# A hybrid decoder layer: the triangular inverse from 16x16 blocks, four gates moved, attention's values channel-major

## The chip, the cores and the metric

The kernel runs on one core of a Trainium2 chip. The metric is the device time of one execution in microseconds (us), as the median of several runs. The engines are TensorE (PE in the profile; its weight loads are PEld), VectorE (DVE), ScalarE (ACT), GpSimd (POOL) and the queue engine SyncE (SP), which issues the loads and stores.

## The reference

One layer, 512 tokens, width 1024, all in fp32:

```python
h = rms_norm(x, norm1_w) * (1 + sc1) + sh1
att_in, rwkv_in, gate_in = split(h @ w_in)
y_att  = attention_mixer(att_in) @ w_att_out
y_rwkv = rwkv7_mixer(rwkv_in, ...) @ w_rwkv_out
g_att, g_rwkv = split(sigmoid(gate_in + b_gate))
x = x + gt1 * ((g_att * y_att + g_rwkv * y_rwkv) @ w_o)
x = x + gt2 * conv_ffn(rms_norm(x, norm2_w) * (1 + sc2) + sh2, ...)
return rms_norm(x, norm_f_w)
```

The attention has 8 heads of 64 channels and three patterns (window and dilation); their results are joined per head by the softmax denominators. In this kernel the patterns are held as two groups: group 0 is the plain window, group 1 both dilated ones. The RWKV mixer has 16 heads of 64 channels. Per token and head its state is multiplied by a decay, corrected by a rank-one term and increased by another; the kernel does this in chunks of 64 tokens, which needs, per chunk and head, the inverse of a unit-triangular 64x64 matrix.

## The kernel before

**Products.** A large product in fp32 is done as three products of rounded halves (hi x hi, hi x lo, lo x hi), each with 512 moving columns. One block of 128 output channels over 1024 inputs is a "body" of 24 such matmuls (`body`). Its weights are loaded, rounded by ACT (`whi`) and the remainder taken by DVE (`wlo`). Small fp32 products run as they are.

**The order of the work.** From the first projections to the end of the mixers the order on each engine is written out by a planner (`Plan.run`, L93). Each task has an engine, an estimated duration, what it depends on, a priority and named buffers that it takes and gives (`take`, `give`). The planner plays the tasks through in time and issues them in that order; on the chip each engine then runs its instructions strictly in that order. Small and urgent PE tasks have low priority numbers (`C_`, `S_`); the units of bodies have `U_` plus their number, so they fill what is left, in the order in which they were made. Bodies write into two PSUM buffers, called `mm`.

**Attention** (`attention`, `attend`). For each block of queries: scores on PE (`sc`), masked minimum on DVE, exponentials on ACT (`pr`), a turn on PE (`pt`), a copy (`pts`), and the product with the values on PE (`po`, function `values`): stationary is the turned probability tile of 128x128, moving are 64 columns of values, so that the result has tokens in partitions. At the end (from L985) each group's share per token and head (`ea`) scales the result on DVE (`scale`, L1017), 32 transposes bring it into channel order and add the two groups in PSUM (`pa<-ident,o`), ACT copies it, and it is stored to `att_d`. During attention DVE also sums up the rest of the conditioning (`ada_rest`: rows of `w_ada` are loaded into `araw` and added into `acc`, L347), and PE adds each sum over the partitions (`ada`).

**The RWKV mixer** (`rwkv`, from L1041). The 16 heads are 8 pairs (`pair`), two pairs make a group, four groups g = 0 to 3. Per group: two pairs, then `inverse(g)`, then `chain(g)` of 8 steps. Pairs of groups 0 and 2 share buffers (`gp0`), and so do 1 and 3 (`gp1`): group 2's pairs start after chain 0 and group 3's after chain 1. Chains follow each other.

**The inverse** (from L1436). Of each 64x64 matrix the two 32x32 diagonal blocks are inverted on DVE for all four blocks and 16 matrices at once: matrices lie in partitions, `turned` transposes, `scaled` multiplies by the inverse norms, and then columns 30 down to 3 are done two at a time (`two`, L1507: a multiply, a reduction and a correction) and the last three singly (`step`, L1500), over rows of up to 32 elements. `rows` and `rows11` turn the result back; two blocks of small matmuls (`first_pe`, `second_pe`, 32 products each of 32x32 with 32 columns, names `pe`) form the off-diagonal block.

**The chain.** In a step, `state` multiplies the carried state (`mbd`) and then the new values with `gt` into `xy`; `state_out` multiplies `mbd` into `xo`; then come solve (`u`), update and output.

**The gates.** 16 bodies (`early_gate`, m = 0 to 15), made after all pairs: the product, a tanh on ACT (`gs`), a store to DRAM (`gate_d`). When all tasks marked `pre` are done (pairs, gates and their stores), `close_pre` closes the pairs' buffers (pool `pp`) and opens those that follow; `gates` (L1818) loads gates 0 to 7 back. After chain 2, `close_even` opens the buffers for `att_out` (L1853): it loads `att_d`, splits it and runs 8 bodies of 12 matmuls (`pa<-ahi,whi` and so on), the results of which are multiplied with gates 0 to 7. `rwkv_ahead` begins the product `pr`. Then follow `rwkv_out`, the mix, and the feed-forward part.

Of the kernel before, what the change touches and what calls it, by code (L numbers as in the profile page):

```python
# [128 lines left out]
class Layer:  # L129
# [502 lines left out]

    def mask2(self):
# [38 lines left out]
    def attention(self):  # L672
# [4 lines left out]
        o = [ap.tile([P, 4, ATT_W], F32, name="o0"), None]  # L677
# [110 lines left out]
        def attend(gi, hf, order, blocks, width, mask, V, ready, prio):  # L788
# [4 lines left out]
            for n, i, new, end in order:  # L793
# [37 lines left out]
                def values(n=n, i=i, d=d, new=new, end=end):  # L831
                    if new:
                        pos[n] = self.aps.tile([P, 256], F32, tag="po", name=self.n("po"), bufs=2)
                    vs = V(n)
                    for h in range(2):
                        cs = slice(i * P + h * 64, i * P + h * 64 + 64)
                        for j, v in enumerate(vs):
                            self.mm(pos[n][:, cs], d["pts"][:, h, j * P : (j + 1) * P], v[:, cs],
                                    new and h == 0 and j == 0, end and h == 1 and j == len(vs) - 1)

                def out(n=n, i=i, new=new):
                    c0, c1 = (i * P if new else 0), i * P + P
                    if gi and o[1] is None:
                        o[1] = ap.tile([P, 4, ATT_W], F32, tag="o1", name="o1")
                    nc.scalar.copy(o[gi][:, n, hf * 256 + c0 : hf * 256 + c1], pos[n][:, c0:c1])
# [11 lines left out]
                t = pe(0.9 * wd / 256, values, [t], S0, take=("po",) if new else (), give=("pts",), name="po")  # L857
# [110 lines left out]
        for _ in ada:  # L968
            pass

# [23 lines left out]
        scaled = []  # L994
        for gi in range(2):
# [19 lines left out]
            def scale(n, gi=gi, ea=ea):  # L1015
                ov = o[gi][:, n, :].rearrange("p (h e) -> p h e", h=8)
                nc.vector.tensor_tensor(ov, ov, ea[:, n, :].unsqueeze(2).to_broadcast([P, 8, 64]), op=ALU.mult)  # L1017
            t = dve(0.6, diff, [got[gi], *stats[gi]], name="al")
            t = sca(0.45, exps, [t], name="al")
            t = dve(1.2, share, [t], name="al")  # L1020
            scaled += [dve(0.7, lambda n=n, scale=scale: scale(n), [t, *outs[gi]], name="al") for n in range(4)]
        for i in range(4):
            d = {}

            def turn(i=i, d=d):
                d["pa"] = self.aps.tile([P, S], F32, tag="pt", name=self.n("pa"), bufs=2)
                for n in range(4):
                    self.tr(d["pa"][:, n * P : (n + 1) * P], o[0][:, n, i * P : (i + 1) * P], n == 0, False)
                for n in range(4):
                    self.tr(d["pa"][:, n::4], o[1][:, n, i * P : (i + 1) * P], False, n == 3)  # L1030

            def out(d=d):
                d["t"] = self.awl.tile([P, S], F32, tag="attT", name=self.n("attT"), bufs=2)
                nc.scalar.copy(d["t"], d["pa"])
            t = pe(0.95, turn, scaled, take=("pt",), name="pa")
            t = sca(0.6, out, [t], take=("attT",), give=("pt",), name="pa")
# [4 lines left out]
    def rwkv(self, tail):  # L1041
# [17 lines left out]
        def half():  # L1059
# [3 lines left out]
                                    op=ALU.add)  # L1063
        self.opened = pl.add("NO", 0, open_, list(pl.tasks), name="open")
# [6 lines left out]
        for g in range(4):  # L1071
# [3 lines left out]
            self.chain(g)  # L1075
        for m in range(2 * KD):
            self.early_gate(m)
# [358 lines left out]
    def inverse(self, g):  # L1436
# [15 lines left out]
        quads = [(e, b, (64 if e == 0 else 0) + 32 * b) for b in range(2) for e in range(2)]  # L1452

# [4 lines left out]
        def recip():  # L1458
            rn = d["rn"] = pp.tile([P, 32], F32, tag="rn", name=self.n("rn"))
            nc.vector.transpose(rn, d["sq"].rearrange("p s y -> p (s y)"))  # L1460
            nc.vector.tensor_scalar(rn, rn, 1e-24, 0.0, op0=ALU.max, op1=ALU.add)
            nc.vector.reciprocal(rn, rn)

        def blocks(j):

            if j == 0:
                d["ld"] = pp.tile([P, 16, 32], F32, tag="lr", name=self.n("ld"))
            e, b, x = quads[j]
            nc.scalar.copy(d["ld"][x : x + 32], blk(e, b, b))

        def turned():
            d["lt"] = pp.tile([P, 32, 32], F32, tag="lt", name=self.n("lt"))
            nc.vector.transpose(d["lt"].rearrange("p j i -> p i j"),
                                d["ld"].rearrange("p y i -> p i y").unsqueeze(2).to_broadcast([P, 32, 2, 16]))

        def scaled():
            lt = d["lt"]
            nc.vector.tensor_tensor(lt, lt, d["rn"].unsqueeze(2).to_broadcast([P, 32, 32]), op=ALU.mult)

        def diagonal():  # L1480
            f = d["lt"].rearrange("p a b -> p (a b)")
            nc.vector.memset(f[:, ::33], 1.0)

            d["sup"] = pp.tile([P, 14], F32, tag="sup", name=self.n("sup"))
            nc.vector.tensor_copy(d["sup"], f[:, 100::66])
            nc.vector.memset(f[:, 100::66], 0.0)

        def first():

            d["both"] = pp.tile([P, 512 + 784], F32, tag="lr", name=self.n("tt"))  # L1490
            f = d["both"][:, :512]
            d["t"] = f.rearrange("p (a b) -> p a b", b=32)
            nc.gpsimd.memset(f, 0.0)
            for x in range(2):
                nc.gpsimd.tensor_scalar(f[:, x : x + 34 * 15 + 1 : 34], d["rn"][:, x::2],
                                        self.half[:, x : x + 1], 0.0, op0=ALU.mult, op1=ALU.add)

        tmp = lambda *n: d["both"][:, 512 : 512 + math.prod(n)]

        def step(j):  # L1500
            n0 = (j + 1) // 2
            sh = [P, 16 - n0, 32 - j]
            t, x = d["t"], tmp(*sh[1:]).rearrange("p (n i) -> p n i", i=32 - j)
            nc.vector.tensor_tensor(x, t[:, n0:, j:], d["lt"][:, j, j:].unsqueeze(1).to_broadcast(sh), op=ALU.mult)
            nc.vector.tensor_reduce(t[:, n0:, j], x, axis=AX.X, op=ALU.add)

        def two(j):  # L1507

            n0 = j // 2
            sh = [P, 16 - n0, 2, 32 - j]  # L1510
            t, x = d["t"], tmp(*sh[1:]).rearrange("p (n c i) -> p n c i", c=2, i=32 - j)
            nc.vector.tensor_tensor(x, t[:, n0:, j:].unsqueeze(2).to_broadcast(sh),
                                    d["lt"][:, j - 1 : j + 1, j:].unsqueeze(1).to_broadcast(sh), op=ALU.mult)
            nc.vector.tensor_reduce(t[:, n0:, j - 1 : j + 1], x, axis=AX.X, op=ALU.add)
            nc.vector.scalar_tensor_tensor(t[:, n0:, j - 1], t[:, n0:, j], d["sup"][:, j // 2 - 2 : j // 2 - 1],
                                           t[:, n0:, j - 1], op0=ALU.mult, op1=ALU.add)

        def rows():

            d["tc"] = tmp(16, 32).rearrange("p (a b) -> p a b", b=32)  # L1520
            nc.vector.transpose(tmp(16, 32).rearrange("p (z y n s) -> p z n s y", z=1, s=2, n=16)[:, 0], d["t"])

        def rows11():

            d["t11"] = d["lt"][:, :16]
            nc.vector.transpose(d["t11"], d["tc"])

# [7 lines left out]
        t = dve(2.06, turned, lds)  # L1535
        t = dve(1.24, scaled, [t, rn])
        t0 = pl.add("POOL", 2.6, first, [t, self.halved], E_)
        t = dve(0.6, diagonal, [t])
        cost = lambda n, j: n * (16 - (j + 1) // 2) * (32 - j) / 480
        t = pl.join([t, t0])  # L1540
        for j in range(30, 2, -2):
            t = dve(0.55 + cost(2, j), lambda j=j: two(j), [t], name=f"inv{g}")
        for j in range(2, -1, -1):
            t = dve(0.37 + cost(1, j), lambda j=j: step(j), [t], name=f"inv{g}")
        tc = dve(1.1, rows, [t], E_)
        t11 = dve(0.72, rows11, [tc], E_)
# [3 lines left out]
        def first_pe():  # L1550
            pe = d["pe"] = self.cps.tile([P, 512], F32, tag="t", name=self.n("pe"))
# [12 lines left out]
        p1 = pl.add("PE", 1.25, first_pe, [t11], 0.5, take=("t",), name="pe")  # L1564
# [7 lines left out]
    def chain(self, g):  # L1572
# [42 lines left out]
        for c in range(NCH):  # L1615
# [9 lines left out]
            def state(c=c, s=s, gt=gt, R=R, X=X, ih=ih):  # L1625
                xy = s["xy"] = ps("xy")
                s["uv"] = uvs[c - c % 2][:, c % 2]
                for i in range(2 if c else 0):
# [49 lines left out]
            so_ = pe(0.33 if c else 0.0, state_out, [st], C_ + 0.01, take=("xo",), name="xo")  # L1678
# [26 lines left out]
        for i in range(2):  # L1705
# [43 lines left out]
            t = pe(1.05, gate, [t, self.sgs], S_, take=("t",), give=("g2",), name="gg")  # L1749
            gt_ = sca(0.6, gate_out, [t], E_, take=("gg",), give=("t",))  # L1750
# [67 lines left out]
    def gates(self, opened):  # L1818
# [4 lines left out]
        def load(m):  # L1823
            self.p[m] = self.pp2.tile([P, S], F32, name=f"gate{m}", tag=f"gate{m}")
            nc.sync.dma_start(self.p[m], self.gd[m])
        for m in range(KD):
# [347 lines left out]
```

## Time and profile before

| | us |
|---|---|
| runs | 1234.05, 1231.15, 1232.48 (median 1232.48) |
| profiled execution | 1231.16 |
| its span, first to last instruction | 1229.4 |
| mean granted clock of TensorE | 0.982 |
| attention, from the first `po` to the last | 77 to 321 |
| chain 0, 1, 2, 3 | 444 to 490, 516 to 560, 644 to 688, 708 to 752 |
| feed-forward, from its first product | 857 |

A row of the timeline has the start, the time and the engine, line, operation and tiles (out<-in) with the shape: for a matmul "128*64 128x512" is the stationary side (rows*columns) and the moving one. In brackets stands the idle time before it and what ended that. A row of the groups ends in the count, the busy time in us, the mean in ns and the idle time before. Matmuls overlap, so the time that one holds PE is the distance to the next start, not its own length.

### The profile page before, as it was taken

The numbers are of one execution on the slowest core, as the hardware profiler recorded it, in microseconds if no ns is written. First come the engines' busy times: TensorE is split into PE (matmuls) and PEld (weight loads), VectorE is DVE, ScalarE is ACT, GpSimd is POOL, SyncE is SP. The second block draws the span as 40 slices with busy tenths as digits, with TensorE's granted clock in tenths as the row PEclk, the third lists the DMA queues.
The fourth block names the chain that finished last, engine by engine and source line by source line (L and its number), as shares of the span: only waits on it lengthen the run. The fifth ranks groups of instructions, "written<-read, shape, count | busy, mean of one in ns | idle before, by whom it ended". The sixth has DMA issues, their size and how long they took to land.

```text
span 1229.4 us, 18443 instructions
## 1 busy us (share of the span) xinstructions
PE 1179.8 (96%) x7188; PEld 946.3 (77%) x7188; DVE 746.0 (61%) x1254; ACT 542.6 (44%) x1009; POOL 120.3 (10%) x235
## 2 busy tenths in 40 slices
PE   4999999999999999999999599999999999999997
PEld 3788888889777876767776467788888888878886
DVE  6687862431678977846896844665556555652135
ACT  4384621522566364464544443444444444442123
POOL 4000000000001013131103122214000000000001
PEclk9899999999999999999999699999999999999999
DMA  9845871130233332413231525560232323333331
GB/s 317 248 142 157 284 236 46 52 86 5 81 100 84 98 108 72 127 44 116 78 99 49 159 60 177 154 206 18 69 103 86 103 86 103 86 103 103 103 120 69
DMA packets 168902, 139.41 MB, mean 113 GB/s; under 512 B 8849, under 2 KB 150251, under 8 KB 168815
## 3 DMA queue, kind: packets, MB, share of 16 engines
q1 hardware_dynamic: 168671, 137.98, 37.0%
q8 instruction: 56, 0.92, 0.3%
q14 instruction: 31, 0.25, 0.1%
q10 hardware_dynamic: 144, 0.26, 0.1%
HBM read 127.65 MB, written 10.56 MB: 112 GB/s over the span
## 4 chain that ended last, share of the span: by engine, by line
PE 82%; DVE 9%; DMA 4%; ACT 2%; issue 1%; SPq 0%; POOL 0%; POOLq 0%; DVEq 0%; ACTq 0%
PE u L148 22%; PE o L148 13%; PE v L148 7%; PE pg L148 7%; PE qk L148 6%; PE pr L148 3%; PE r L148 3%; PE k L148 3%; PE pa L148 3%; DMA araw<-in_w_ada_dram 2%; PE early L148 2%; PE po L148 2%; PE xy L148 2%; PE pt L151 1%; PE xo L148 1%
## 5 line engine op out<-in xcount | busy, mean ns | idle before, releaser
L194 DVE TENSOR_TENSOR wlo<-raw,whi 128x1024 fp32r<-128x1024 f32 x67 | 83.9, 1252 | 152.6 <-ACT whi L193 152.6
L148 PE MATMUL u<-h2lo,whi 128*128 128x512 f32 (+2 forms) x368 | 142.3, 387 | 0.0
L148 PE MATMUL u<-h2hi,whi 128*128 128x512 f32 (+2 forms) x368 | 142.2, 387 | 0.0
L148 PE MATMUL u<-h2hi,wlo 128*128 128x512 f32 (+2 forms) x368 | 142.2, 386 | 0.0
L1136 ACT CAST whi<-raw 128x1024 fp32r<-128x1024 f32 (+2 forms) x73 | 72.5, 994 | 122.7 <-PE qk L148 49.5
L193 ACT CAST whi<-raw 128x1024 fp32r<-128x1024 f32 x67 | 70.3, 1049 | 112.1 <-PE o L148 53.8
L1139 DVE TENSOR_TENSOR wlo<-raw,whi 128x1024 fp32r<-128x1024 f32 (+2 forms) x73 | 83.7, 1149 | 19.1 <-ACT whi L1136 18.8
L148 PEld LDWEIGHTS u<-h2lo,whi 128*128 128x128 f32 x368 | 68.9, 187 | 15.8 <-POOL h2lo L405 0.2
L148 PEld LDWEIGHTS u<-h2hi,wlo 128*128 128x128 f32 x368 | 68.9, 187 | 15.7
L148 PEld LDWEIGHTS u<-h2hi,whi 128*128 128x128 f32 x368 | 68.9, 187 | 15.4
L2019 DVE SCALAR_TENSOR_TENSOR u<-u,cols,u 128x511 f32<-128x511 f32 x88 | 65.7, 746 | 4.3 <-ACT u L2017 2.7
L148 PE MATMUL qk<-hhi,wlo 128*128 128x512 f32 x160 | 64.0, 400 | 0.0
L148 PE MATMUL qk<-hlo,whi 128*128 128x512 f32 x160 | 63.6, 397 | 0.0
L148 PE MATMUL qk<-hhi,whi 128*128 128x512 f32 x160 | 63.5, 397 | 0.0
L148 PE MATMUL o<-whi,fhi 128*128 128x512 f32 x144 | 56.1, 390 | 0.3 <-DVE u L2019 0.3
L148 PE MATMUL o<-whi,flo 128*128 128x512 f32 x144 | 56.0, 389 | 0.0
L148 PE MATMUL o<-wlo,fhi 128*128 128x512 f32 x144 | 56.0, 389 | 0.0
L148 PE MATMUL pg<-hhi,wlo 128*128 128x512 f32 x128 | 51.8, 405 | 0.0
L148 PE MATMUL pg<-hlo,whi 128*128 128x512 f32 x128 | 51.7, 404 | 0.0
L148 PE MATMUL pg<-hhi,whi 128*128 128x512 f32 x128 | 51.7, 404 | 0.0
L810 DVE CUSTOM_DVE_ANT_0 sm<-sc,m 128x256 f32<-128x256 f32 (+1 forms) x64 | 23.9, 404 | 37.6 <-PE sc L148 36.5
L347 DVE SCALAR_TENSOR_TENSOR acc<-araw,cols,acc 128x1024 f32<-128x1024 f32 x28 | 35.9, 1281 | 15.9 <-DMA araw<-in_w_ada_dram 15.8
(409 smaller groups left out, 2779.1 us busy)
## 6 DMA issues: line engine op xcount, KB each, us to landing
raw<-in_w_in_dram SPq DMA_DIRECT2D x62, 512.0 KB
raw<-in_w_up_dram SPq DMA_DIRECT2D x44, 512.0 KB
araw<-in_w_ada_dram SPq DMA_DIRECT2D x32, 512.0 KB
raw<-in_w_down_dram SPq DMA_DIRECT2D x22, 512.0 KB
araw<-in_w_ada_dram SPq DMA_DIRECT2D x32, 256.0 KB
wvraw<-in_w_in_dram SPq DMA_DIRECT2D x20, 256.0 KB
gate_d<-gs SPq DMA_DIRECT2D x16, 256.0 KB
gate<-gate_d SPq DMA_DIRECT2D x16, 256.0 KB
```

Of the source, the lines that this page charges most:

```text
L148: return self.nc.tensor.matmul(out, lhsT, rhs, start=start, stop=stop)
L151: self.nc.tensor.matmul(out, in_, self.ident[: in_.shape[0], : in_.shape[0]], is_transpose=True, start=start, stop=stop,)
L193: self.nc.scalar.copy(hl[0], raw)
L194: (lo_eng or self.nc.vector).tensor_tensor(hl[1], raw, hl[0], op=ALU.subtract)
L347: nc.vector.scalar_tensor_tensor(d["acc"], raw, ck, d["acc"], op0=ALU.mult, op1=ALU.add)
L810: nc.vector.tensor_tensor_reduce(d["sm", h][:, :wd], d["sc"][h][:, :wd], m[:, 256 - wd : 256] if gi == 0 else m[:, :wd], 1.0, 3.0e38, op0= ...
L1136: nc.scalar.copy(d["w"][0], d["raw"])
L1139: nc.vector.tensor_tensor(d["w"][1], d["raw"], d["w"][0], op=ALU.subtract)
L2019: nc.vector.scalar_tensor_tensor(u[:, d:], pu[:, : S - d], ch(c), u[:, d:], op0=ALU.mult, op1=ALU.add)
```

## The change

It has four parts.

**The inverse.** DVE now inverts the four 16x16 diagonal blocks of each 64x64 matrix. `two` runs six times (columns 14 to 4) and `step` three times, over at most 16 elements. `turned` handles half as many elements. Two blocks of 64 products each (`half_pe`, 32x32 stationary with 16 moving columns), each followed by an ACT copy, and a further transpose join them to 32x32 blocks; then `first_pe` and `second_pe` follow as before.

```diff
-        for j in range(30, 2, -2):
-            t = dve(0.55 + cost(2, j), lambda j=j: two(j), [t], name=f"inv{g}")
+        for j in range(14, 2, -2):
+            t = dve(0.55 + 2 * (16 - j) ** 2 / 480, lambda j=j: two(j), [t], name=f"inv{g}")
...
-        t11 = dve(0.72, rows11, [tc], E_)
+        t = [dve(0.27, wide0, [t], E_), sca(0.42, wide1, [t], E_)]
+        tc = dve(1.1, rows, t, E_)
+        t = dve(0.72, rows11, [tc], E_)
+        for j in range(2):
+            t = pl.add("PE", 1.6, lambda j=j: half_pe(j), [t, ey], 0.5, take=() if j else ("t",), name="pe")
+            tc = t = sca(0.42, lambda j=j: half_out(j), [t], 0.5, name="pe")
+        t11 = dve(0.72, rows11, [tc], 0.5)
...
+        def half_pe(j):
...
+            for y in range(16):
+                for e, b, x in quads:
+                    r = slice(x, x + 32)
+                    l, t = (part("lr", 512, 32)[r, y], d["tc"][r, y, 16:]) if j else (blk(e, b, b)[:, y], d["t11"][r, y, :16])
+                    self.mm(d["pe"][r, 256 * j + 16 * y : 256 * j + 16 * y + 16], l, t, y == 0, y == 15)
```

**Four gates.** Gates 4 to 7 are no early gates any more. Their bodies are made in `gates`, after all others of the pairs, and ACT writes them into their last place once the pairs' buffers are closed; the store and the load fall away.

```diff
+        self.late = range(4, KD)
         for m in range(2 * KD):
-            self.early_gate(m)
+            if m not in self.late:
+                self.early_gate(m)
...
+            if m in self.late:
+                t, d = self.body("gate", self.gate_w(m), KD, "mm", lambda: self.mmp("pg"), self.hT)
+                self.pt[m] = self.pl.add("ACT", 0.7, lambda m=m, d=d: here(m, d), [t, opened], E_, give=("mm",))
+            else:
...
```

**The state in one go.** In `state` the products with `gt` come first and those with `mbd` last, and `state_out` has the highest priority behind them. The gate of `chain` takes its buffer `gg` with the product instead of with the copy.

```diff
                 for i in range(2 if c else 0):
-                    self.mm(xy[X[i], :P], prs[i]["ar"][:, c, X[i]], mbd(i), True, False)
-                for i, h, cs, ci in ih:
-                    self.mm(xy[X[i], cs], gt(i, h, R[i], X[i]), s["uv"][R[i], ci], c == 0 and h == 0, h == 1)
+                    self.mm(xy[X[i], :P], prs[i]["ar"][:, c, X[i]], mbd(i), False, True)
...
-            so_ = pe(0.33 if c else 0.0, state_out, [st], C_ + 0.01, take=("xo",), name="xo")
+            so_ = pe(0.24 if c else 0.0, state_out, [st], C_ - 1.0, take=("xo",), name="xo")
```

**Attention's values.** `values` has 64 columns of values stationary and the 128 probabilities moving, the two heads in the two halves of the partitions, so the result comes out with channels in partitions. The shares per token and head are turned on PE, split in two halves (`hi`, `lo`) and spread over the 64 channels of each head by a product with a pattern of ones (`share_rows`, written by POOL); DVE multiplies, POOL adds the two groups, and the 32 transposes and the ACT copies at the end fall away.

```diff
-                            self.mm(pos[n][:, cs], d["pts"][:, h, j * P : (j + 1) * P], v[:, cs],
-                                    new and h == 0 and j == 0, end and h == 1 and j == len(vs) - 1)
+                    for j, v in enumerate(vs):
+                        for h in range(2):
+                            c0 = i * P + h * 64
+                            self.mm(pos[n][h * 64 : h * 64 + 64, i * P : i * P + P], v[:, c0 : c0 + 64],
+                                    d["pts"][:, h, j * P : (j + 1) * P], new and j == 0, end and j == len(vs) - 1)
...
+            def turn(gi, i=i, d=d):
+
+                d["w", gi] = self.aps.tile([P, S], F32, tag="pt", name=self.n("pw"), bufs=2)
+                self.mm(d["w", gi], self.heads[:, i * P : (i + 1) * P], self.share[gi], True, True)
...
+                nc.gpsimd.tensor_tensor(d["t"], o[0][:, i, :], o[1][:, i, :].rearrange("p (r j) -> p j r", r=4), op=ALU.add)
```

More of the change, by code (lines that the diff above doesn't have):

```diff
@@ L631, in masks, with share_rows @@
                 pattern=[[-1, P]], channel_multiplier=1)
+    def share_rows(self):
+        nc = self.nc
+        self.heads = self.awl.tile([P, 2, S], F32R, tag="qk12", name="heads", bufs=1)[:40, 0, :]
+        t = self.awl.tile([P, 2, S], F32R, tag="qk02", name="share", bufs=1)[:40]
+        self.share = [t[:, gi, :] for gi in range(2)]
+        one = lambda r, c: self.ident[r, c : c + 8].unsqueeze(2).to_broadcast([r.stop - r.start, 8, 64])
+        h = self.heads.rearrange("p (h e) -> p h e", e=64)
+        for r, c in ((slice(0, 32), 0), (slice(32, 40), 32)):
+            nc.gpsimd.tensor_copy(h[r], one(r, c))
+        for x in self.share:
+            nc.gpsimd.tensor_copy(x[:32].rearrange("p (h e) -> p h e", e=64), one(slice(0, 32), 64))
     def mask2(self):
@@ L969, in attention @@
             pass
+        heads = pl.add("POOL", 3.0, self.share_rows, sc, E_, take=("qk02", "qk12"), name="heads")
         def pre():
@@ new lines, in attention, with turn, hi, lo @@
+        parts = []
+        for gi in range(2):
+            d = {}
+            def turn(gi=gi, d=d):
+                d["ps"] = self.aps.tile([P, S], F32, tag="pt", name=self.n("pe"), bufs=2)
+                for n in range(4):
+                    self.tr(d["ps"][:8, n * P : (n + 1) * P], shares[gi][1][:, n, :], n == 0, n == 3)
+            def hi(gi=gi, d=d):
+                nc.scalar.copy(self.share[gi][:8], d["ps"][:8])
+            def lo(gi=gi, d=d):
+                nc.vector.tensor_tensor(self.share[gi][32:40], d["ps"][:8], self.share[gi][:8], op=ALU.subtract)
+            t = pe(0.48, turn, [shares[gi][0], heads], take=("pt",), name="pa")
+            t = sca(0.6, hi, [t], name="pa")
+            parts.append(dve(0.7, lo, [t], give=("pt",), name="pa"))
@@ L1037, in attention @@
+            t = pl.add("POOL", 1.2, out, ts, E_, take=("attT",), name="pa")
             pl.add("DMA", 0.8, lambda i=i, d=d: nc.sync.dma_start(self.att_d[:, i, :], d["t"]), [t], W_, lag=2.0,
@@ L1452, in inverse @@
         quads = [(e, b, (64 if e == 0 else 0) + 32 * b) for b in range(2) for e in range(2)]
+        a0, a1 = [lambda s=s: self.half[:, s : s + 1] for s in range(2)]
+        part = lambda t, c, n: d[t][:, c : c + 16 * n].rearrange("p (y n) -> p y n", n=n)
         def norms():
@@ L1507, in two @@
-        def two(j):
[L1509 to L1516, printed above, removed]
+            sh = [P, 15 - j, 16 - j]
```

148 lines of the change are left out of this document (83 added, 65 removed).

## The prediction

> **What bounds the kernel now.** I read the page's share by engine and its slices first, then the windows, the timeline around the one hole, and the groups by shape.
>
> ```profile
> span 1229.4 us, 18443 instructions
> PE 1179.8 (96%) x7188; PEld 946.3 (77%) x7188; DVE 746.0 (61%) x1254; ACT 542.6 (44%) x1009; POOL 120.3 (10%) x235
> PE   4999999999999999999999599999999999999997
> PEclk9899999999999999999999699999999999999999
> ```
>
> TensorE (PE) is full in every slice but the first, the last and number 23, where the granted clock falls too. So a microsecond counts only if it is PE work, or falls into a hole of PE. Two windows size that hole (columns: us, busy PE, PEld, DVE, ACT, POOL, clock, DMA share, GB/s):
>
> ```profile
> 682.00:712.00 30.00, 16.89 (x213) 12.20 (x215) 24.01 (x43) 13.34 (x29) 3.93 (x5) 0.54 0.63 184
> 712.00:742.00 30.00, 30.00 (x298) 19.96 (x298) 12.29 (x26) 13.27 (x39) 7.85 (x16) 1.00 0.16 45
> ```
>
> Between 682 and 712 us PE is busy 16.89 us at a clock of 0.54, which is 16.89 x 0.54 = 9.1 us of full-clock work: 30 - 9.1 = 20.9 us are lost. The rows of that place say why (timeline, and the rows of single lines and tiles):
>
> ```profile
> L1816 ACT ACTIVATE gs<-pg,b_gate x16: 674/682/693, 425.2 to 681.3; 128x512 f32<-128x512 f32 x16
> 655.00:697.20 42.20, 0.00 (x0) 0.00 (x0) 22.06 (x50) 2.47 (x4) 1.47 (x3) 0.85 0.35 111
> L1841 SPq DMA_DIRECT2D ld<-att_d x4: 319/375/430, 685.2 to 698.0; - x4
> 687.92 0.97 PE L148 MATMUL xo<-uv,gt 128*64 128x64 f32 x8 [0.36 <-ACT uv L1654]
> 693.31 0.48 PE L151 MATMUL t<-ident,yt 128*128 128x128 f32 x1 [3.58 <-POOL yt L1801]
> 705.82 1.12 PE L148 MATMUL u<-cen,v 128*64 128x128 f32 x8 [3.03 <-DVE u L1589]
> 706.87 0.80 PE L148 MATMUL pa<-ahi,whi 128*128 128x512 f32 x1
> ```
>
> The last of the 16 early gates is evicted at 681.3; they were the filler of PE. The inverse of group 3 occupies VectorE until 697 (second row: instructions on tile tt alone, 22.06 us of DVE), so chain 3 begins only at 705.8, though chain 2 issued its last products at 687.9. The output projection of attention (pa) needs its loads, issued 685.2 to 698.0, and begins at 706.9, 19 us after chain 2. Three suppliers fail at once.
>
> **The change part by part.** All times are against the profiled execution, 1231.16 us: its span of 1229.4 and 1.8 around it. The median of the three runs, 1232.48, lies 1.3 above.
>
> *Late gates and shorter inverse: the hole.* Rows by shape for the inverse, and a gate's pace:
>
> ```profile
> L1473 DVE STREAM_TRANSPOSE lt<-ld 128x1024 f32<-128x1024 f32 x4 | 8.1, 2037 | 1.2 <-ACT ld L1469 1.2
> L1512 DVE TENSOR_TENSOR tt<-tt,lt 128x256 f32<-128x256 f32 x4 | 1.7, 425 | 0.1
> L1514 DVE TENSOR_REDUCE tt<-tt 128x16 f32<-128x256 f32 x4 | 1.7, 421 | 0.1
> L1515 DVE SCALAR_TENSOR_TENSOR tt<-tt,sup 128x10 f32<-128x10 f32 x4 | 1.0, 238 | 0.1
> L1512 DVE TENSOR_TENSOR tt<-tt,lt 128x4 f32<-128x4 f32 x4 | 0.6, 160 | 0.1
> 433.14 0.39 PE L148 MATMUL pg<-hhi,whi 128*128 128x512 f32 x1
> 433.37 0.39 PE L148 MATMUL pg<-hlo,whi 128*128 128x512 f32 x1
> ```
>
> The 14 steps of two columns and 3 single ones shrink from up to 784 elements to at most 288: six steps of two and three single ones. From the rows (0.16 us at 4 elements, 0.425 at 256) a multiply averages 0.28, a reduction the same, the correction 0.24: 6 x (0.28 + 0.28 + 0.24) + 3 x 2 x 0.37 = 7.0 us, against some 20 of the 22.06 (two closing transposes are in it). The first transpose, over 1024 elements, halves (-1), the scaling after it loses a third of its 1.2 and the extra small ones add 1.5. DVE is left with about 12 us per inverse where it had 25 (22.06 + 2.04 + the scaling); the new round trips (two blocks of matmuls, two ACT copies, one more transpose) give back some 5 of latency. Each inverse ends about 8 us sooner, and chain 3 can follow chain 2 at once. A gate is 24 matmuls at 0.23 us = 5.5; four of them, 22 us of PE work, now run without a store and a load and do not hold back the moment when the pairs' buffers close. Eight DMA issues leave SP. In the gap of some 19 us from chain 2's end to pa there are now chain 3 and up to 22 us of gates. I count 19 of the 20.9 us as won. What is late next is nothing on that path: PE work itself. Bounds: 0 to -21.
>
> *Joining the 16x16 blocks.* Eight new blocks of 64 products each, fp32, so 128 matmul records (this trace shows two records for each fp32 product). Nearest row, the existing joining step with 32 products:
>
> ```profile
> 433.96 1.20 PE L148 MATMUL pe<-lt,gt 32*32 32x32 f32 x64 [0.20 <-DVE lt L1526]
> 435.09 0.50 PE L148 MATMUL pg<-hhi,wlo 128*128 128x512 f32 x1
> ```
>
> 64 records hold PE for 435.09 - 433.96 = 1.13 us. Half as wide a moving side (16) could halve that, or not touch it; four positions instead of two could overlap, or not. Full price by records: 8 x 2 x 1.13 = 18.1, less the 8 x 0.13 of setting up that a block pays once = 17. Low end: 128 records in the time of 64, 8 x 1.13 = 9. I take 17, the row as it stands, and 2 us more for waits (each block waits for DVE or ACT; the 0.20 in the row is one such wait). The Trainium skill, "TensorE: Matmul & The Clock Gate", section "Wait — 56ns, not 53.3ns?", states that start-to-start stays at or above about 25 ns however narrow the moving side is; by it 16 columns cost what 32 cost and the term is 17, which speaks against this part. No row here has 16 columns.
>
> *Attention's values.* Stationary and moving sides change places: 128x64 against 128x128, the two heads in different column halves. That shape exists already (u<-cen,v):
>
> ```profile
> 317.19 1.00 PE L148 MATMUL po<-v,pts 128*128 128x64 f32 x8
> 318.00 0.47 PE L148 MATMUL lg<-hhi,whi 128*128 128x512 f32 x1
> 642.28 0.66 PE L148 MATMUL u<-cen,v 128*64 128x128 f32 x8
> 642.86 0.50 PE L148 MATMUL pg<-hlo,whi 128*128 128x512 f32 x1
> 60.00:186.00 126.00, 14.43 (x112) 14.60 (x112) 4.27 (x16) 1.00 0.65 203
> 179.84 3.95 DMA araw<-in_w_ada_dram
> 185.23 1.08 PE L148 MATMUL ada<-acc,ones 128*1 128x256 f32 x4 [2.09 <-DVE acc L347]
> L151 PE MATMUL pa<-ident,o 128*128 128x128 f32 x32 | 3.9, 276 | 0.2 <-DVE o L1017 0.2
> L1911 POOL TENSOR_TENSOR gate<-gate,gate 128x512 f32<-128x512 f32 x8 | 11.2, 1408 | 41.4 <-DVE gate L1910 41.4
> ```
>
> 0.81 us become 0.58: 0.23 per eight records, 240 records in all, -6.9. But 112 of them run before 186 us (fifth row, tile po), where PE waits for the conditioning vector's sums anyway, and these hang on DMA (the load of 3.95 us ends 183.8); half of that share, 1.5, may only lengthen the wait. I take -5.4 (bounds -2 to -7). The 32 transposes of the end (3.9 us, 0.12 each) give way to 8 narrow ones (1.0 at the same price) and 8 products of 512 columns (0.23 each, with 0.1 for the interruption, 2.6): -0.3. At attention's end stand one more turn and four adds on POOL (nearest row 1.41 us each, last row) where ACT copied; the heads' pattern is written by POOL earlier. The pairs open up to 4 us later; early gates and projections that wait for nothing cover that, and without the cover it costs those 4.
>
> *State in one go.* The matmuls with mbd come after those with gt, next to state_out's. First a step 0, which has no mbd, then a full step as it is now:
>
> ```profile
> 643.96 0.45 PE L148 MATMUL xy<-uv,gt 64*64 64x64 f32 x8
> 644.34 0.66 PE L151 MATMUL pt<-ident,bk 128*128 128x128 f32 x4
> 649.04 0.44 PE L148 MATMUL xy<-mbd,ar 128*64 128x128 f32 x4
> 649.41 0.45 PE L148 MATMUL xy<-uv,gt 64*64 64x64 f32 x8
> 649.79 0.44 PE L148 MATMUL xo<-mbd,ar 128*64 128x128 f32 x4
> 650.16 1.16 PE L148 MATMUL pg<-ar,bk 64*128 64x128 f32 x16
> ```
>
> A full step is 650.16 - 649.04 = 1.12. Afterwards it is 0.38 for the eight with gt (644.34 - 643.96) and, as for u<-cen,v, 0.58 for eight of 128x128: 0.96. At 28 steps -4.5 at best, 0 at worst; I take -3. That the gt products no longer queue behind the wait for mbd shortens the chain, but the chain does not set the end.
>
> **Sum:** -19 + 17 + 2 - 5.4 - 0.3 - 3 = -8.7; 1231.2 - 8.7 = 1222.5.
>
> **The rivals.**
>
> *Cheap joining.* The four positions run side by side and a block costs 9/8 us: 8 us less, 1214. For it: the rows are in different 32x32 positions. Against: in the row with two positions 64 records still take 1.13, and the two records of one product follow each other on one position. The Trainium skill, "TensorEngine Tiling (Array Packing)", Key Properties, has different tiles work in parallel, which would give this case. Chance 0.18.
>
> *The hole half returns.* Twelve gates run out before chain 2 ends, or two late gates hold both projection buffers of PSUM until the pairs close. PE then has only the chain for some 9 us. 1222.5 + 9.5 = 1232. Against it: the inverses of groups 0 and 2 on the way to chain 2's end are 8 us shorter each, so 16 us less filler is needed before. Chance 0.1.
>
> *Slower: the hole stays and the joining is paid in full.* Waits of PE at the blocks today:
>
> ```profile
> PE pe L148 <- DVE lt L1567: 1.4, 1, 1.4
> PE pe L148 <- DVE y L1765: 1.1, 1, 1.1
> PE pe L148 <- DVE lt L1526: 0.4, 2, 0.2
> ```
>
> If pa's loads still end 19 us after chain 2 and chain 3 is held by the inverse's new round trips, the first term is 0: 1222.5 + 19 = 1241.5. It decides where the blocks' ACT copies and waits eat more than the 13 us that DVE saves per inverse; each of the five new steps of that way would have to take 2.6 us. For it: in-order PE runs what is queued ahead of each block. Against: these waits total 2.9 us for all eight blocks, mostly inside the hole. Chance 0.13.
>
> **How the numbers follow.** Forecast 0.55 (own range 1215 to 1229: the bounds of joining, values and state taken half each), cheap joining 0.18, half hole 0.1, slower 0.13, and 0.04 for what I do not see. A difference within 0.2% (2.5 us) is about what a measurement of this kernel can tell from none, so faster is below 1230: nearly all of the forecast, cheap joining and a part of the half hole, 0.77; same 0.09; slower 0.14. The range takes in cheap joining with the other bounds (1209) and the half hole with its spread (1236), leaving out most of the slower case.
>
> **What would show it.** In the profile after: no slice of PE below 9 but the ends, clock 1.0 around chain 3; pg rows inside chain 3; DVE on the inverse near 12 us per group; a pe block of 128 records at about 2.1 us; eight po records at 0.58; a step's state at 0.96. Wrong if a hole of over 5 us stands between the last early gate and pa, or if the blocks take 1.1 us or over 2.5.

## The result, and the profile after

The changed kernel takes 1242.48 us (median of 6 runs, 1238.41 to 1246.29), the kernel before 1233.26 beside it (6 runs): ratio 1.0077, 95% interval 1.006 to 1.0094. It is slower by some 9 us where 1222.5 was forecast; the time lies above the range too.

The page of the changed kernel, its share by engine and its slices:

```profile
span 1239.3 us, 20413 instructions
PE 1192.2 (96%) x8196; PEld 939.8 (76%) x8196; DVE 704.8 (57%) x1181; ACT 547.0 (44%) x1019; POOL 124.8 (10%) x243
PE   4999999999999999999899999999999999999997
PEclk9899999999999899999899999999999999999999
q8 instruction: 64, 1.05, 0.4%
```

The hole did close: slice 23 is full and at full clock. But there is an 8 in slice 20, the clock dips in slices 14 and 20 instead, and PE has 1008 matmuls more. Two windows of the old place, in the changed kernel (us, then busy time of PE, PEld, DVE, ACT and POOL, the clock, DMA share, GB/s):

```profile
682.00:712.00 30.00, 29.83 (x294) 20.47 (x293) 10.72 (x25) 13.40 (x39) 7.95 (x18) 1.00 0.21 58
712.00:742.00 30.00, 29.92 (x209) 22.30 (x208) 16.98 (x28) 15.96 (x35) 5.86 (x8) 1.00 0.57 176
```

Of 60 us only 0.25 are lost there, where before lost 20.9 of the first 30. The loss has moved. Four windows of 14 us, one around the two new blocks of each group, first in the changed kernel:

```profile
416.00:430.00 14.00, 12.64 (x403) 9.82 (x404) 9.02 (x13) 6.74 (x11) 0.11 (x1) 0.76 0.33 87
471.00:485.00 14.00, 12.09 (x456) 9.38 (x452) 2.33 (x7) 5.52 (x14) 2.06 (x4) 0.88 0.22 75
608.00:622.00 14.00, 10.03 (x346) 8.03 (x346) 6.10 (x10) 5.85 (x11) 0.96 (x2) 0.76 0.12 34
660.00:674.00 14.00, 11.27 (x400) 8.65 (x400) 2.80 (x7) 6.46 (x16) 2.53 (x5) 0.88 0.01 4
```

Busy time by clock gives 9.6, 10.6, 7.6 and 9.9 us of full-clock work, so 18.2 of the 56 us are lost. The timeline's rows of the new blocks show on what (start, time, operation, count of records; in brackets the idle time ahead and what ended it):

```profile
415.92 1.26 PE L148 MATMUL pe<-lr,gt 32*32 32x16 f32 x128
417.11 0.50 PE L148 MATMUL v<-hlo,whi 128*128 128x512 f32 x1
...
418.24 0.83 PE L148 MATMUL pe<-lt,lr 32*32 32x16 f32 x77
420.42 0.61 PE L148 MATMUL pe<-lt,lr 32*32 32x16 f32 x51 [1.36 <-issue]
...
473.65 0.39 PE L148 MATMUL pe<-lt,lr 32*32 32x16 f32 x25
475.95 1.10 PE L148 MATMUL pe<-lt,lr 32*32 32x16 f32 x103 [1.91 <-issue]
...
612.08 1.23 PE L148 MATMUL pe<-lt,lr 32*32 32x16 f32 x127 [1.23 <-ACT cs L1340]
616.05 0.18 PE L148 MATMUL pe<-lt,lr 32*32 32x16 f32 x1 [2.74 <-issue]
...
667.33 0.24 PE L148 MATMUL pe<-lt,lr 32*32 32x16 f32 x5 [2.35 <-issue]
```

The first new block holds PE for 417.11 - 415.92 = 1.19 us. The second stops in its middle, after record 77, 25, 127 and 123, for 8.4 us in all; "issue" means that PE waited for nothing that the profile shows. Behind three of the stops the granted clock is 0.5 for 3.4 or 6.8 us (that is what 0.88 and 0.76 of 14 us are). In group 2 it falls at 613.33 us, as the stop begins, behind the wait of 1.23 us for ACT that stands ahead of the block, and stays at 0.5 for 6.8 us. So about as much PE time is lost as before, at four new places, and the work has grown.

**Two theories.** *Instruction supply:* queue 8 moved 64 packets, 1.05 MB, so 16.4 KB each; PE's 8196 matmuls and 8196 weight loads over 64 packets are 256 instructions a packet. A new block is 128 records (64 products) with a weight load each, exactly one packet, in 1.2 us. If packets can't follow each other that fast, PE runs dry. The packets of queue 8 around two of the stalls (from the trace, start in us; each took 0.88 to 1.31):

```
group 0:  404.06   418.20   422.12   425.87   436.06
group 2:  582.89   609.31   613.35   617.20   624.09
```

In the joining they start 3.75 to 4.04 us apart, and PE resumes 2.2 and 2.7 us after the packets of 418.20 and 613.35. In group 0 the 256th instruction ahead of the stall runs at 416.60 us, the packet starts at 418.20 and ends at 419.16, and PE resumes at 420.42. *Rival:* the second block itself is slow, by its operands, its positions in the array, or the transfers of weights beside it.

### The profile page after: what moved, and what is told of

Same layout as the page of the kernel before. It is cut to its first block, busy times and chain, and to the rows that moved or that the text cites. A ratio compares the mean times of both kernels' runs of the same rounds, so it can differ in the third digit from the quotient of the medians.

```text
span 1239.3 us, 20413 instructions
## 1 busy us (share of the span) xinstructions
PE 1192.2 (96%) x8196; PEld 939.8 (76%) x8196; DVE 704.8 (57%) x1181; ACT 547.0 (44%) x1019; POOL 124.8 (10%) x243
## 3 DMA queue, kind: packets, MB, share of 16 engines
q8 instruction: 64, 1.05, 0.4%
## 4 chain that ended last, share of the span: by engine, by line
PE 86%; DVE 5%; issue 3%; DMA 3%; ACT 2%; POOL 1%; SPq 0%; POOLq 0%; DVEq 0%; ACTq 0%
PE u L148 22%; PE o L148 13%; PE pg L148 10%; PE qk L148 7%; PE v L148 7%; PE k L148 4%; PE r L148 3%; PE pa L148 2%; PE xy L148 2%; PE early L148 2%; DMA araw<-in_w_ada_dram 2%; PE pr L148 2%; PE pe L148 2%; PE pt L151 1%; PE sc L148 1%
## 5 line engine op out<-in xcount | busy, mean ns | idle before, releaser
L148 PE MATMUL o<-whi,fhi 128*128 128x512 f32 x144 | 56.1, 390 | 0.3 <-DVE u L2098 0.3
L148 PE MATMUL pg<-hlo,whi 128*128 128x512 f32 x128 | 55.2, 431 | 0.0
L148 PE MATMUL pg<-hhi,whi 128*128 128x512 f32 x128 | 54.5, 426 | 0.0
L148 PE MATMUL pg<-hhi,wlo 128*128 128x512 f32 x128 | 53.5, 418 | 0.0
```

Source lines behind the costliest of these rows:

```text
L148: return self.nc.tensor.matmul(out, lhsT, rhs, start=start, stop=stop)
```

## The experiments

Ratios are to the kernel before, run on the same chip.

**1. The blocks spread out (spread).** Four tasks of 16 products for each block, with a pause in the planner in which bodies run:

```diff
-            t = pl.add("PE", 1.6, lambda j=j: half_pe(j), [t, ey], 0.5, take=() if j else ("t",), name="pe")
+            for q in range(4):
+                t = pl.add("PE", 0.30, lambda j=j, q=q: half_pe(j, q), [t, ey], 0.5, take=() if j or q else ("t",),
+                           name="pe", lag=1.5 if q < 3 else 0.0)
...
-            for y in range(16):
+            for y in range(4 * q, 4 * q + 4):
```

> The changed kernel (1242.5 us) with each of the two new blocks of 64 products cut into four tasks of 16, 1.5 us apart in the planner, so that products of bodies lie between them. Nothing is left out. Theory (instruction supply): PE's instructions arrive in packets of 16 KB, that is 256 instructions, on queue 8, and in the joining two packets start at least 3.5 us apart, while the two blocks issue 512 instructions in 2 x 1.2 us; PE runs dry. Then the four stalls (8.7 us in all) go, the granted clock of 0.5 behind them (20.4 us of it, some 6 us lost) goes too, and 24 more interruptions at 0.2 us cost 4.8: about 1242.5 - 8.7 - 6 + 4.8 = 1232.6, between 1228 and 1236. Rival (the second block's own operands or array positions are slow): the same total of stalls, spread over the four tasks, 1242 to 1247.

Measured: 1225.47 us, ratio 0.9944 (0.9924 to 0.9963), faster than both kernels. Timeline rows of group 0 and the same four windows, in spread:

```profile
423.95 0.44 PE L148 MATMUL pe<-lt,lr 32*32 32x16 f32 x32
426.00 0.44 PE L148 MATMUL pe<-lt,lr 32*32 32x16 f32 x32
427.69 0.44 PE L148 MATMUL pe<-lt,lr 32*32 32x16 f32 x32
429.34 0.44 PE L148 MATMUL pe<-lt,lr 32*32 32x16 f32 x32
```

```profile
416.00:430.00 14.00, 14.00 (x307) 10.69 (x307) 10.06 (x14) 7.40 (x13) 0.43 (x2) 1.00 0.40 107
471.00:485.00 14.00, 14.00 (x311) 10.10 (x300) 2.35 (x6) 5.33 (x17) 2.54 (x5) 1.00 0.27 77
608.00:622.00 14.00, 14.00 (x278) 10.66 (x277) 9.93 (x15) 7.29 (x12) 0.93 (x2) 1.00 0.27 75
660.00:674.00 14.00, 14.00 (x312) 9.96 (x314) 2.85 (x8) 4.73 (x15) 4.33 (x8) 1.00 0.32 96
```

No stall and no dip of the clock: the same 1024 records, in the same positions, with the same operands, lose nothing. The 18.2 us of the windows come back nearly whole (1.0077 - 0.9944 = 0.0133, 16.4 us). My expectation was too high by 7 us, because more came back than I had put. Call PE's idle time and half of its busy time at half clock its loss, and the rest of the span its full-clock work. From 60 us on the loss falls from 39.0 us to 17.3, by 21.7 where I had put 8.7 + 6. The full-clock work rises from 1178.2 us to 1184.0, by 5.8, which is near the 4.8 that I had put for the interruptions.

**2. The first block left out (no_first).** The products of `half_pe(0)` are skipped and ACT copies `t11` in their place.

> The changed kernel with the first of the two new blocks left out (its products; ACT copies the transposed 16x16 inverse in their place), so the inverse is not the reference's. The second block stays as it was. Theory (instruction supply): with 256 instructions fewer in the burst the second block of 128 records runs in 1.2 us without a stall, and the clock stays at 1.0 behind it: 1242.5 - 4.8 - 8.7 - 6 = 1223, 1219 to 1227. Rival (the second block's own operands): its four stalls of about 2.2 us stay, 1242.5 - 4.8 = 1237.7, 1235 to 1240.

Measured: 1227.58 us, ratio 0.9968 (0.9949 to 0.9987), 0.6 us above the range of the supply theory and 7 below that of the rival. Timeline rows of groups 0 and 3:

```profile
415.15 1.26 PE L148 MATMUL pe<-lt,lr 32*32 32x16 f32 x128
...
650.29 1.21 PE L148 MATMUL pe<-lt,lr 32*32 32x16 f32 x123
653.09 0.24 PE L148 MATMUL pe<-lt,lr 32*32 32x16 f32 x5 [1.58 <-issue]
```

Three of the four second blocks run through, so their operands are not slow. The fourth still stops, and again after record 123: leaving out exactly four packets ahead of it doesn't move the border. In group 2 a stall of 1.3 us has left the block for the body behind it. A packet's worth in 1.2 us is enough to run dry where the border falls badly. The clock is still 0.5 for 13.7 us in three places around the blocks, one of them behind a wait of 1.1 us for DVE, so not all of the half clock is the packets' doing.

**3. The borders moved (phase).** 64 more instructions of PE at 320 us, some 100 us ahead of the first stall:

```diff
                 d["ps"] = self.aps.tile([P, S], F32, tag="pt", name=self.n("pe"), bufs=2)
+                for _ in range(16 * (gi == 0)):
+                    self.mm(d["ps"][:8, :8], self.ident[:8, :8], self.ident[:8, :8], True, True)
```

> The changed kernel with 16 additional products of 8x8 by 8 (32 records, 64 instructions of PE) at the end of attention, about 320 us; their result is not used. If the stalls stand at the borders of the 256-instruction packets, each moves by 32 records towards the front: from record 77, 25, 127 and 123 of the second block to 45, ahead of the block (25 - 32 is negative: the stall, or most of it, ends at the block's first record or in the bodies just ahead), 95 and 91, and the packets on queue 8 still start at least 3.5 us apart there. Rival (something in the block itself, or the weights' DMA running beside it): the stalls stay where they were, at 77, 25, 127 and 123. The time stays within 4 us of the changed kernel's.

Timeline rows of the four groups:

```profile
418.78 0.56 PE L148 MATMUL pe<-lt,lr 32*32 32x16 f32 x45
420.51 1.01 PE L148 MATMUL pe<-lt,lr 32*32 32x16 f32 x83 [1.18 <-issue]
...
474.64 0.33 PE L148 MATMUL u<-xs,gt 64*64 64x64 f32 x3 [2.95 <-issue]
475.83 1.83 PE L148 MATMUL pe<-lt,lr 32*32 32x16 f32 x121
478.74 0.30 PE L148 MATMUL pe<-lt,lr 32*32 32x16 f32 x7 [1.08 <-issue]
...
612.89 0.98 PE L148 MATMUL pe<-lt,lr 32*32 32x16 f32 x95
615.09 0.44 PE L148 MATMUL pe<-lt,lr 32*32 32x16 f32 x33 [1.22 <-issue]
...
662.23 0.94 PE L148 MATMUL pe<-lt,lr 32*32 32x16 f32 x91
664.15 0.49 PE L148 MATMUL pe<-lt,lr 32*32 32x16 f32 x37 [0.98 <-issue]
```

The stalls stand after records 45, 95 and 91, each 32 earlier, and the one of group 1 has left the block and sits ahead of it, in a product of the chain (`u`). Group 1 has a second stall, which I had not expected, after record 121 of its block: that is 128 records, one packet, behind the first. It is one run, 1237.24 us, 5.2 under the changed kernel's median, a little more than the 4 expected: the five stalls are 7.4 us in all, where four were 8.4. Counted over all instructions of PE in the traces, the 15 stalls of over 0.9 us that are put down to "issue" in this kernel, the changed one, no_first, no_late and spread2 (below) all stand at the same place modulo 256, behind the 193rd instruction. That settles the supply; the weights' transfers beside a block don't move with 64 instructions of PE.

**4. Two tasks for each block (spread2, spread2_all).** As spread, with tasks of 32 products, 2 us apart (`lag=2.0 if q < 1 else 0.0`), and then with 2.2 us behind every task but the last, also between the two blocks (`lag=0.0 if q and j else 2.2`).

> As spread (1225.5 us), but each new block cut into two tasks of 32 products (128 instructions), 2 us apart in the planner, instead of four. Nothing is left out. The supply of 256 instructions per 3.5 to 3.9 us is kept if bodies fill the time between; then 16 interruptions fewer at 0.1 to 0.2 us: 1225.5 - 2.4 = 1223, 1221 to 1225. Rival (two tasks of 128 instructions and the bodies between them come faster than the packets): stalls of 1 to 2 us in the second block return with a half clock behind them, 1228 to 1238.

> As spread2 (1227.1 us), with 2.2 us kept in the planner behind every task of the joining but the last, also between the first block and the second, where spread2 had three tasks of 128 instructions within 5 us and one stall of 1.4 us with a further half-empty time behind it. Nothing is left out. Theory (instruction supply): no stall is left, 1227.1 - 1.4 and some 1 to 2 us behind it: 1224.5, 1222 to 1226, the same as spread with 16 interruptions fewer. Rival (the stall of spread2 has another cause): 1226 to 1229 with a stall in one of the groups.

Measured: 1227.10 us, ratio 0.9954 (0.9938 to 0.9969), and 1226.62, 0.9948 (0.9932 to 0.9963). Group 1 of spread2:

```profile
476.02 0.78 PE L148 MATMUL pe<-lr,gt 32*32 32x16 f32 x64
477.69 0.73 PE L148 MATMUL pe<-lt,lr 32*32 32x16 f32 x64
480.90 0.37 PE L148 MATMUL pe<-lt,lr 32*32 32x16 f32 x22
482.62 0.53 PE L148 MATMUL pe<-lt,lr 32*32 32x16 f32 x42 [1.35 <-issue]
```

Three tasks of 128 instructions within 5 us bring one stall back; with the second pause no stall is left. The times of the two and of spread can't be told apart, and the 16 interruptions saved show no gain: I had expected 1221 to 1225 and 1222 to 1226, and both came out higher, spread2 with the rival's stall but not its time (1228 to 1238).

**5. Parts undone and alone.** The other gates and the old inverse, each put back into the changed kernel: `self.late = range(0)` (no_late), and the whole function `inverse` of before, without the small pattern that only the new one uses (old_inv). A form of old_inv that kept this pattern (old_inverse) needed more on-chip memory than there is and gave no time.

> The changed kernel with all 16 gates early again, as before; the rest of the change stays. If the late gates are what closed the hole of 682 to 712 us, it comes back by 5 to 15 us of lost PE time and the time is 1247 to 1257. If the shorter inverse closes it alone, the time stays within 1239 to 1246. Rival (the late gates' interruptions of chain 3 cost more than they fill): 1233 to 1238.

> The changed kernel with the inverse of before (32x32 blocks on VectorE, no new blocks on PE) and without the small pattern that only the new one uses; four late gates, state in one go and channel-major values stay. Theory (the joining is what made it slower): without 9.5 us of blocks, 8.7 of stalls and some 6 of half clock it falls to 1218, if the late gates alone keep PE busy around chain 3; each us of the hole that comes back adds one, up to 20 (1238). I expect 1222, 1216 to 1230, faster than the kernel before. Rival (another part, the late gates or the values, made it slower): 1238 or more.

Measured: no_late 1257.22 us, ratio 1.0198 (1.0155 to 1.0241); old_inv 1239.26, 1.0043 (1.0024 to 1.0061). PE's slices and one wait of no_late, then PE's slices of old_inv:

```profile
PE   4899999999999999999899969999999999999997
...
PE t L151 <- DVE y L1837: 10.3, 1, 10.3
```

```profile
PE   4999999999999999899999699999999999999997
```

A 6 stands in slice 24 of the one and 23 of the other: the hole is back. (In old_inv there is an 8 in slice 17 too; by busy time and clock it loses 7.8 us between 500 and 600 us, spread 1.2.) With early gates alone PE has no filler when chain 3 hands on its outputs (10.3 us in one wait); with the old inverse alone four late gates aren't enough. My expectation for old_inv (1222) was wrong: I took the late gates as enough. Each of the two needs the other.

The chain of after in the kernel before (state_only), and the attention of after in the kernel before (values_only):

> The kernel before with nothing but the new chain (state in one go). The forecast took 0.16 us off each of 28 steps, but at most 3 us in all, chain 3 lying at the hole: 1231 - 3 = 1228, 1226.5 to 1231. If the order of the products in a step doesn't matter: 1231.

> The kernel before with nothing but the new attention (values channel-major, shares spread by a product). The trace of the changed kernel has 17.9 us for the products with the values where before has 25.0, and 3.9 for the end of attention as before: 7 us less on PE, of which the forecast counted 5.4. If PE's work sets the end, 1231 - 7 = 1224 (1223 to 1227). Rival (the saving before 186 us, and the pairs' later opening, give it back): 1228 to 1231.

Measured: 1245.49 us, ratio 1.0105 (1.008 to 1.0129), and 1240.31, 1.006 (1.0042 to 1.0078). Both were expected to be faster (1226.5 to 1231, and 1223 to 1227 or at most 1231), and both are slower. Windows of 660 to 800 us, first before, then values_only:

```profile
660.00:700.00 40.00, 30.35 (x327) 20.63 (x324) 34.16 (x77) 16.72 (x42) 12.24 (x20) 0.81 0.40 122
700.00:740.00 40.00, 36.10 (x366) 24.32 (x366) 18.41 (x37) 17.97 (x50) 7.85 (x16) 0.85 0.27 76
740.00:800.00 60.00, 57.00 (x323) 43.42 (x322) 35.36 (x44) 23.57 (x38) 14.07 (x14) 1.00 0.54 167
```

```profile
660.00:700.00 40.00, 30.07 (x280) 21.09 (x279) 30.65 (x75) 15.75 (x44) 13.62 (x24) 0.68 0.39 124
700.00:740.00 40.00, 37.79 (x371) 26.71 (x369) 25.71 (x46) 19.60 (x44) 4.89 (x9) 0.94 0.32 94
740.00:800.00 60.00, 52.20 (x346) 37.32 (x346) 26.82 (x39) 20.70 (x42) 17.95 (x20) 0.91 0.39 125
```

By busy time and clock, before loses 15.4 + 9.3 + 3.0 = 27.7 us there and values_only 19.6 + 4.5 + 12.5 = 36.6: 9 more, where the kernel is 7 slower. Its full-clock work is 1166.8 us, just as much as before, so the 7 us saved on the products don't show there either (see "The hole" below). For state_only the same sum is 27; 7 more are lost between 500 and 600 us. From 60 us on it loses 53.5 us where before loses 40.8, which is the 13 by which it is slower; what moved these waits was not followed.

**6. Parts undone where the hole and the stalls are gone.** In spread, the chain of before, the attention of before, and both new blocks without their products (ACT copies `t11`):

> As spread (1225.5 us), with the chain of before (the state's products in the old order). With the hole closed PE's work sets the end, so the term of the forecast shows: 3 us (bounds 0 to 4.5). The sums of the starts of xy and xo in the two traces differ by 2: 1228, 1226 to 1230. If the part costs more than it saves: under 1225.

> As spread (1225.5 us), with the attention of before (values token-major, 32 transposes at the end). The two traces have 25.0 us against 17.9 for the products with the values, and 3.8 against 3.9 for the end: 7 us of PE work come back, less 0 to 1.5 that before 186 us only fill a wait: 1232, 1230 to 1233. By the forecast's term 5.7: 1231. If saved PE work ahead of the chains isn't kept, as in the kernel before: 1218 to 1226.

> As spread (1225.5 us), with the products of the two new blocks left out (ACT copies the transposed 16x16 inverse in their place), so the inverse is not the reference's; the planner's order stays. The difference is what the joining costs PE once its supply keeps up. From the starts in spread's trace: 32 tasks of 0.37 us = 11.8, and 0.1 more for each interruption, 15 in all: 1210.5, 1207 to 1213. By the forecast (17 and 2): 1206.5. By the rival of cheap joining (9): 1216.5.

Measured: 1226.88 us, ratio 0.9955 (0.994 to 0.997); 1232.03, 1.0006 (0.9987 to 1.0024); 1217.51, 0.9872 (0.9838 to 0.9905). Against spread's 0.9944 the state in one go is worth 1.4 us, inside the noise; the values 7.6; and joining, when its instructions arrive in time, costs 8.9 (4 to 14 by the two intervals). Of the expectations, those for the chain (1226 to 1230) and the attention (1230 to 1233) held; for the joining I had expected 1207 to 1213, and it came out cheaper, near the rival's 1216.5.

## Why the prediction was wrong

**The step that failed** is the sentence behind the first term: "What is late next is nothing on that path: PE work itself." What was late next was PE's own instructions. I looked for what PE would wait for among engines, buffers and transfers, and priced the new blocks as work alone; that 256 instructions in 1.2 us follow another 256 by about 2 us appears nowhere in the sum. Its price was 16.4 us (13 to 20) by the ratios of the changed kernel and spread, of the 20 by which the forecast missed; in it is also the wait of 1.23 us for ACT in group 2, with its half clock, which spread doesn't have. The rest is two terms that went wrong in opposite directions: the hole gave some 12 less than I counted and the joining cost 10 less than its 17 + 2; the forecast also starts 2 us below the 1233.26 of the kernel before. With the stalls gone the time is 1225.5, inside the forecast's own range of 1215 to 1229, though not by the terms it gave, as follows.

**The joining's price** was mis-sized. I took 17 us, eight blocks of 128 records at 2.1; a block takes 1.19, so that halving the moving side, or using four positions instead of two, halved a record. Eight blocks are 9.5, and 8.9 was measured (profiled executions: 1225.27 - 1213.10 = 12.2). The rival of cheap joining had the right price (9, 9/8 us a block) and its time of 1214 failed on the same missing term. The Trainium skill, "TensorE: Matmul & The Clock Gate", section "Wait — 56ns, not 53.3ns?", by which I had given a second reason for 17, doesn't hold for these blocks: 1.19 us over 128 records is 9.3 ns from start to start, not the 25 or more that it states. The row that I priced by was below it already, 1.13 us over 64 records being 17.7 ns; and 128 records at 25 ns would have made 25.6 us for eight blocks, not 17. The 0.13 us taken off a block for setting up stands in no row; a piece of 32 records in spread holds PE for 0.37 us, which with 1.19 for 128 gives about 0.10.

**The hole.** That late gates and a shorter inverse together close it was right, and its place loses 0.25 us in 60. Both were needed: undoing the gates costs 14.9 us (1.0198 - 1.0077), undoing the inverse 12.2 from spread (1.0043 - 0.9944), net of the joining and with what it loses at 500 to 600 us. But the terms don't add up as I added them. Without the joining I had 27.7 us of gain (19 + 5.4 + 0.3 + 3); spread_no_join has 15.8 (12 to 20). The values and the state gave 9.0 where 8.7 was forecast, so the hole is short by some 12. The traces show where it went. From 60 us on PE loses 40.8 us to idle time and half clock in before and 19.3 in spread_no_join, so some 21 were won; but its full-clock work is 1166.8 us and 1171.5, where the forecast had the values and the state take 8.7 off. One part of that work is the time by which matmuls of 512 columns hold PE beyond 0.227 us (the distance to the next start, counted up to 0.35, at full clock, from 60 us on): 43.6 us in before, 56.1 in spread_no_join and 57.6 in spread. An interrupted body pays at its edges (417.11 - 415.92 is the block alone; the matmul behind it then takes 0.33 instead of 0.23, as the row of 417.11 and the next start, 417.44, show), and what closes a hole is a body that is interrupted. But half of the rise goes with the values: 50.7 in spread_old_values, and 50.6 in values_only, where it eats the 7 us saved. That the closed hole brought the other half is argued and not shown, and why the values bring theirs stays open.

**Values and state.** 5.7 and 3 were forecast, 7.6 and 1.4 measured where they can act. Rows of the timeline, the first two of the changed kernel, the next four of spread:

```profile
317.63 0.66 PE L148 MATMUL po<-pts,v 128*64 128x128 f32 x8
318.22 0.42 PE L148 MATMUL lg<-hhi,wlo 128*32 128x512 f32 x1
```

```profile
691.50 0.45 PE L148 MATMUL xy<-uv,gt 64*64 64x64 f32 x8
691.88 0.44 PE L148 MATMUL xy<-mbd,ar 128*64 128x128 f32 x4
692.15 0.39 PE L148 MATMUL xo<-mbd,ar 128*64 128x128 f32 x4
692.46 0.50 PE L148 MATMUL pg<-hlo,whi 128*128 128x512 f32 x1
```

Eight po records hold PE for 0.59 us (0.58 forecast) and a step's state 0.96, as forecast; where another product comes between, as in many steps, it doesn't.

**The slower rival** (the hole stays and the joining is paid in full, 1241.5) has almost the measured time and the wrong mechanism: neither happened. What came is its counterpart: the joining paid in stalls, as much as the hole had cost. The check "wrong if the blocks take 1.1 us or over 2.5" did its work: the first block takes 1.19, the second 2.7 to 4.1 with its stall.

## What to carry to other kernels

Ask of every burst of small matmuls how many instructions it has, not only how long it runs: here a stalled PE had the next packet of 256 some 3 to 4.5 us after it began on the one before, while 64 small fp32 products (128 records, each with its weight load) use one up in 1.2. Cut such a burst into pieces of 64 to 128 instructions and put long matmuls between them; the same records then cost 8.9 us, where run in one go they cost some 25 (1.0077 - 0.9872). And judge parts by undoing them in the version in which nothing else is in the way: here two parts that gain 7.6 us and 1.4 (the second inside the noise) in the spread kernel made the old kernel slower by 7 and 13.

## What the runs showed of the hardware

A PE that runs out of instructions shows as idle time put down to "issue" in the middle of one group of matmuls. From the 256th instruction ahead of a stall to the instruction that ends it the traces have 2.8 to 4.5 us (one of 6.1). In group 0 the packet starts 1.6 us behind that instruction. Both are in keeping with a packet that is asked for when 256 instructions are left. The Trainium skill, "Advanced Engine Details and Errata", section "ISA Cache", gives lines of 16 KB, 256 instructions, and two of them; these runs agree with both. It gives TensorE 128 KB as well, which would be eight such lines; with that much ahead PE should not run dry 256 instructions behind the border at which the missing packet was asked for, and here it does. The Trainium skill, "Runtime: NRT & Kernel Launch", section "Instruction fetch mechanics", has the crossing of such a border mostly hidden: so it is in spread, where long matmuls lie around the border, and in the changed kernel each of four cost 1.4 to 2.7 us.

Idle times far shorter than the 3.4 us of half clock that follow them can bring the clock down: 1.36 us idle in the changed kernel gave 6.8 us at 0.5, 1.18 in phase 3.4; 0.98 there and 1.35 in spread2 gave none. The Trainium skill, "TensorE: Matmul & The Clock Gate", section "HAM oscillation — how this bites in real kernels", gives as its rule no idle gaps of over about 3.4 us; by these runs a third of that can be enough.
